# Mixers of a two-block transformer kernel on one core: the first dilated pair ahead of the last two delta heads

## The chip, the cores and the metric

One Trainium2 chip, one of its cores. The metric is the device time of one execution in microseconds (us). The kernel is built once and runs as one program.

## What is computed

The reference runs two blocks on a sequence of 1024 tokens of width 1024. The first has two hybrid layers (retention, neighbourhood attention, short convolution). The second, which the change touches, mixes tokens in two ways at once, and a projection, a normalisation and a feed-forward follow.

```python
h = rmsnorm(x, g_mix_pre)
proj = h @ w_in
qa, ka, va, gate_a, beta_a, alpha_a, qb, kb, vb = split(proj)
out_a = gated_deltanet(qa, ka, va, gate_a, beta_a, alpha_a, ...)   # 4 heads of 128
out_b = dilated_attention(qb, kb, vb, rel_bias)                    # 8 heads of 64, in 4 pairs
mix = concatenate([out_a, out_b]) @ w_out
x = x + rmsnorm(mix, g_mix_post)
```

A delta head takes its q, k and v through a causal convolution over 4 tokens and silu, normalises q and k, solves a triangular system in each chunk (t_inv), then runs a recurrence over the chunks (v_new, o_i, state), and is multiplied by silu of its gate at the end. A dilated pair is two heads of softmax attention under a mask and a bias.

## The kernel before

All matrices are fp32. Each projection splits both operands into a rounded fp32r part and a remainder and adds three products (`xh,wh`, `xl,wh`, `xh,wl`). The names: `xh`/`xl` are the hidden state, `wh`/`wl` a weight.

A **projection block** is `fm_block`: one 128-wide column block of `w_in` against all tokens, two groups of 24 matmuls with 512 columns, so 48 matmuls of one length. The mixers make 24 of them, in the order of the string `ORDER`. An item `c0` is delta head 0: three blocks (k, v, q), each followed by the convolution of that block (`conv_gen`, tiles `c2x`, `c2y`, mostly VectorE), and then the head itself, `gdn_gen`. An item `d0` is dilated pair 0: a block for keys (`dK`), a block for queries (`dQ`), then eight units (`dil_unit`). An item `g0` is the gate of delta head 0: one block, multiplied onto the finished head (`g2o`).

`gdn_gen` of a head is called here in three parts: the *recursion* (31 pairs of a VectorE multiply into `Tt` and a VectorE reduction into `T`, each of which needs the one before), the *solve* (some 120 small fp32 matmuls and their evictions: `Y`, `Z`, `YT`, `gk`, `gv`, `kbe`), and the *scan* over 8 chunks (`vn`, `Sg`: TensorE and VectorE in turns). A `dil_unit` computes scores (TensorE), adds bias `dB` and takes the maximum while reading PSUM (VectorE, the tile `dsl`), exponentiates (ScalarE), scales (VectorE), transposes (TensorE), splits the transposed block (`pt`: ScalarE, then VectorE) and multiplies with the values `dv` (TensorE).

The engines run their rows strictly in the order in which they stand. That order is set when the kernel is built: `Mixer` holds a clock of its own, steps the waiting generators (heads, units, convolutions) between the matmuls of the projection blocks, and gives each row a rank. So `ORDER` decides in which projection blocks a head or a unit can be interleaved. `ROOM` and `need_room` wait for free tiles before a pair starts; `need2` makes the gate of a head wait for the head.

Weights are fetched two blocks ahead by SyncE's queue (`wr`), split by ScalarE (`wh`) and GpSimd (`wl`), in the same order as the blocks (`weights2` reads `ORDER` too). After the mixers `after_mix` multiplies with `w_out` (first rows: `wh,yhl`).

Of the kernel before, what the change touches and what calls it, by code (L numbers as in the profile page):

```python
# [1679 lines left out]
class Block2(Layers):  # L1680
# [18 lines left out]
    def weights2(self):  # L1699
        io = self.io  # L1700
        self.down_weights(io["w_vb2"], self.token_groups(0))
        w = io["w_in2"]
        for s in self.ORDER.split():
            i = int(s[1])
# [46 lines left out]
    def mixers(self, hT):  # L1751
# [23 lines left out]
        self.left = {}  # L1775
        order = self.ORDER.split()
        for n, s in enumerate(order):
# [23 lines left out]
                self.gate2_block(i, gx)  # L1801
        self.free(*hT.tiles())

    ORDER = "c0 c1 c2 c3 d0 g0 d1 g1 d2 d3 g2 g3"
    ROOM = 6
    CG = 4
    CA = 3
# [884 lines left out]
```

## Time and profile before

| | us |
|---|---|
| median of 3 runs | 2977.12 (2975.47 to 2979.05) |
| the profiled execution | 2977.17 |
| its span, first to last instruction | 2975.4 |
| TensorE busy in the span | 2724.7 (92%) |
| VectorE busy in the span | 1999.8 (67%) |
| the mixers' stretch of the span | 1552 to 2174 |

The span is what the trace shows; 1.8 us lie around it. The granted TensorE clock is given as a share of full speed; a stretch at 0.5 ran at 1.2 GHz, one at 1.0 at 2.4 GHz, and values between are means over both. Busy TensorE at half clock does half the work.

### The profile page before, as it was taken

Reading aid. Unit: us, or ns where it says so; the run is one execution under the profiler, and the core shown is the slowest. Engines: PE = TensorE matmul, PEld = TensorE weight load, DVE = VectorE, ACT = ScalarE, POOL = GpSimd, SP = SyncE. Lnnn points to the kernel's source line nnn. Section 1 sums busy time; section 2 is a strip of 40 time slices with the busy share of each in tenths; the row PEclk is TensorE's granted clock in tenths of the full one; section 3 lists DMA queues with packets and bytes.
Section 4 is the critical chain, followed back from the end, with each engine's and each line's share of the span. In section 5 each row is a group of like instructions: output and inputs, shape, how many; then the busy total and the mean of one; then the engine's idle time right before and its main releaser. Section 6 shows DMA issues by size and latency. Waiting matters only on the chain. (4 is left out here: it accounts for less than half of the span.)

```text
span 2975.4 us, 41142 instructions
## 1 busy us (share of the span) xinstructions
PE 2724.7 (92%) x14508; PEld 2340.2 (79%) x14508; DVE 1999.8 (67%) x3985; ACT 1200.1 (40%) x2745; POOL 975.0 (33%) x830
## 2 busy tenths in 40 slices
PE   6989999999879989999889968798998799999997
PEld 6978888888779878888787757687776688887885
DVE  7866776684642557665554887777744877876786
ACT  5222254553442225554444323455544333333443
POOL 4343512213443441222563321110135644443001
PEclk9989999999989999999999979998998899999998
DMA  7534202225333221224543433221353122223874
GB/s 268 178 101 120 91 24 89 78 76 198 114 99 102 64 68 36 95 81 142 171 131 117 162 130 116 86 86 53 107 170 137 69 106 107 107 106 143 299 234 156
DMA packets 170480, 358.44 MB, mean 120 GB/s; under 512 B 29761, under 2 KB 57697, under 8 KB 170273
## 3 DMA queue, kind: packets, MB, share of 16 engines
q1 hardware_dynamic: 157472, 333.63, 33.2%
q10 hardware_dynamic: 10016, 13.12, 1.8%
q0 software_dynamic: 2784, 9.05, 1.0%
q8 instruction: 115, 1.88, 0.3%
q14 instruction: 93, 0.75, 0.1%
HBM read 274.11 MB, written 75.32 MB: 117 GB/s over the span
## 5 line engine op out<-in xcount | busy, mean ns | idle before, releaser
L251 POOL TENSOR_TENSOR wl<-wr,wh 128x512 fp32r<-128x512 f32 (+2 forms) x344 | 459.3, 1339 | 1177.9 <-ACT wh L251 1086.3
L344 PE MATMUL pb<-xl,wh 128*128 128x512 f32 x1456 | 579.7, 398 | 0.0
L344 PE MATMUL pb<-xh,wl 128*128 128x512 f32 x1456 | 579.1, 398 | 0.0
L344 PE MATMUL pb<-xh,wh 128*128 128x512 f32 x1456 | 578.9, 398 | 0.0
L251 ACT ACTIVATE wh<-wr 128x512 fp32r<-128x512 f32 (+2 forms) x344 | 203.6, 594 | 419.1 <-PE pb L344 331.0
L344 PEld LDWEIGHTS pb<-xh,wl 128*128 128x128 f32 x1456 | 277.6, 191 | 56.0 <-issue 0.6
L344 PEld LDWEIGHTS pb<-xl,wh 128*128 128x128 f32 x1456 | 278.0, 191 | 54.7 <-issue 0.2
L344 PEld LDWEIGHTS pb<-xh,wh 128*128 128x128 f32 x1456 | 277.9, 191 | 53.3 <-issue 0.3
L344 PE MATMUL pb<-wh,yhl 128*128 128x512 f32 x832 | 267.9, 401 | 15.8 <-DVE lr L251 6.9
L344 PE MATMUL pb<-T,wh 128*128 128x512 f32 x640 | 198.0, 391 | 15.3 <-DVE T L251 15.3
L344 PEld LDWEIGHTS pb<-wh,yhl 128*128 128x128 f32 x832 | 160.6, 194 | 51.4 <-issue 8.0
L251 POOL TENSOR_TENSOR wl<-ws,wh 128x512 fp32r<-128x512 f32 x100 | 137.1, 1371 | 137.7 <-ACT wh L251 133.8
L344 PE MATMUL pb<-wl,yhl 128*128 128x512 f32 x416 | 166.4, 400 | 6.3 <-POOL wl L251 6.3
L344 PE MATMUL pb<-whi,yhl 128*128 128x512 f32 x528 | 163.8, 391 | 4.5 <-DVE yhl L251 4.5
L251 ACT ACTIVATE pt<-pb 128x512 fp32r<-128x512 f32 (+3 forms) x230 | 114.9, 528 | 123.8 <-PE pb L349 121.7
L251 DVE TENSOR_TENSOR pt<-pb,pt 128x512 fp32r<-128x512 f32 (+3 forms) x230 | 129.4, 595 | 51.2 <-ACT pt L251 50.5
L344 PEld LDWEIGHTS pb<-T,wh 128*128 128x128 f32 x640 | 120.5, 189 | 40.8 <-DVE T L251 15.7
L251 DVE TENSOR_TENSOR yhl<-yr,yhl 128x512 fp32r<-128x512 f32 (+2 forms) x133 | 99.1, 771 | 60.0 <-ACT yhl L251 59.6
L344 PE MATMUL pb<-wl,xh 128*128 128x384 f32 (+1 forms) x384 | 126.3, 329 | 6.5 <-POOL wl L251 6.5
L251 ACT ACTIVATE wh<-ws 128x512 fp32r<-128x512 f32 x100 | 63.2, 632 | 168.4 <-PE pb L344 167.6
L344 PE MATMUL pb<-wh,xl 128*128 128x384 f32 (+1 forms) x384 | 125.4, 327 | 3.3 <-ACT wh L251 1.4
L344 PE MATMUL pb<-T,wl 128*128 128x512 f32 x320 | 125.0, 390 | 0.0
(432 smaller groups left out, 6020.8 us busy)
## 6 DMA issues: line engine op xcount, KB each, us to landing
wr<-in_w_in_dram SPq DMA_DIRECT2D x152, 256.0 KB, 2.7
ws<-in_w_down_dram SPq DMA_DIRECT2D x110, 256.0 KB, 5.0
wr<-in_w_out_dram SPq DMA_DIRECT2D x96, 256.0 KB, 2.9
yr<-ffn SPq DMA_DIRECT2D x33, 512.0 KB, 5.9
wm<-in_w_modT_dram SPq DMA_DIRECT2D x32, 512.0 KB, 4.3
wr<-in_w_v_dram SPq DMA_DIRECT2D x64, 192.0 KB, 2.4
ws<-in_w_gate_dram SPq DMA_DIRECT2D x22, 512.0 KB, 5.2
ws<-in_w_up_dram SPq DMA_DIRECT2D x22, 512.0 KB, 5.6
```

Source lines behind the costliest of these rows:

```text
L251: return fn(*a, **kw)
L344: self.mix.product(c / 2.4, out, (lhsT, rhs), lambda: self.nc.tensor.matmul(out, lhsT, rhs, start=start, stop=stop))
```

## The change

The order of the items changes, and nothing else: pair 0 comes after two delta heads instead of after four. `weights2` reads the same string, so that the weights come in the new order too.

```diff
-    ORDER = "c0 c1 c2 c3 d0 g0 d1 g1 d2 d3 g2 g3"
+    ORDER = "c0 c1 d0 c2 c3 g0 d1 g1 d2 d3 g2 g3"
```

Each engine keeps the same matmuls and evictions; 11891 printed rows stand on TensorE in both programs. The first six blocks (c0, c1) are where they were. Three places show what moved.

**VectorE, at the start of head 0's recursion** (`T`, `Tt`; `c2y` is a convolution, `dK` the keys of pair 0, `rr` a norm of head 1). Before:

```order
L251 TENSOR_SCALAR rr_3315_16212<-pb_16203 128x8
L251 TENSOR_TENSOR rr_3315_16212<-rr_3315_16212,egc 128x8
L251 SCALAR_TENSOR_TENSOR c2y_16093<-c2x_16092,conv_13771,c2y_16093 128x1023
L251 COPY T_16303<-tini 128x256
L251 SCALAR_TENSOR_TENSOR c2y_16093<-c2x_16092,conv_13771,c2y_16093 128x1022
L251 TENSOR_TENSOR Tt_16305<-T_16303,nd_16164 128x8x2
L251 SCALAR_TENSOR_TENSOR c2y_16093<-c2x_16092,conv_13771,c2y_16093 128x1021
L251 TENSOR_REDUCE T_16303<-Tt_16305 128x8
```

And in the changed kernel:

```order
L251 TENSOR_SCALAR rr_3315_16211<-pb_16202 128x8
L251 TENSOR_TENSOR rr_3315_16211<-rr_3315_16211,egc 128x8
L251 TENSOR_TENSOR dK_3297_16092<-pb_16106,dK_3297_16092 64x512
L251 TENSOR_TENSOR dK_3298_16093<-pb_16106,dK_3298_16093 64x512
L251 TENSOR_TENSOR dK_3297_16092<-pb_16187,dK_3297_16092 64x512
L251 TENSOR_TENSOR dK_3298_16093<-pb_16187,dK_3298_16093 64x512
L251 COPY T_16309<-tini 128x256
L251 TENSOR_TENSOR Tt_16311<-T_16309,nd_16164 128x8x2
L251 TENSOR_REDUCE T_16309<-Tt_16311 128x8
```

The convolutions of heads 2 and 3 left this place and pair 0's keys came to it. From the copy into `T` to the first score of pair 0 there are now 60 of the recursion's 62 rows, 1 row of a convolution, 4 of `dQ`, 4 of `dv`, 5 of the heads and 1 of `dB`.

**TensorE, after head 1's first products** (`gq`, `gk`). Before, projections of head 2 follow:

```order
L344 MATMUL pb_16438<-gq_16273,gk_16271 128x128 x4
L344 MATMUL pb_16453<-gk_16271 128x128 x4
L344 MATMUL pb_16454<-gq_16273,gk_16271 128x128 x4
L344 MATMUL pb_16405<-xl_14687,wh_16338 128x512
L344 MATMUL pb_16405<-xh_14683,wh_16338 128x512
L344 MATMUL pb_16405<-xh_14683,wl_16339 128x512
```

In the changed kernel the scores of pair 0 follow, 16 rows of them, and then its transpositions:

```order
L344 MATMUL pb_16386<-gq_16277,gk_16275 128x128 x4
L344 MATMUL pb_16405<-gk_16275 128x128 x4
L344 MATMUL pb_16406<-gq_16277,gk_16275 128x128 x4
L344 MATMUL pb_16429<-dK_3297_16092,dQ_3316_16229 128x512
L344 MATMUL pb_16429<-dK_3297_16092,dQ_3318_16231 128x512
L344 MATMUL pb_16438<-dK_3297_16092,dQ_3316_16229 128x512
L344 MATMUL pb_16438<-dK_3297_16092,dQ_3318_16231 128x512
```

No projection stands between the heads' products and the scores, and the next projections (head 2's) come behind the first values of the pair.

**TensorE, at the mixers' end** (`wh,yhl` is the output projection's first matmul, `pb_21036` in the rows of before the last gate's projection). Before:

```order
L344 MATMUL pb_21036<-xl_14688,wh_20836 128x512
L344 MATMUL pb_21036<-xh_14684,wh_20836 128x512
L344 MATMUL pb_21036<-xh_14684,wl_20837 128x512
L344 MATMUL pb_21073<-pt_21053,dv_20428 128x256 x2
L344 MATMUL pb_21073<-pt_21053,dv_20428 128x128 x2
L344 MATMUL pb_21086<-wh_20842,yhl_21095 128x512
```

In the changed kernel:

```order
L344 MATMUL pb_21053<-pt_21010,dv_20428 128x256 x2
L344 MATMUL pb_21053<-pt_21010,dv_20428 128x128 x2
L349 MATMUL pb_21066<-ident,dsl_21028 128x128 x3
L344 MATMUL pb_21073<-pt_21070,dv_20428 128x256 x2
L344 MATMUL pb_21073<-pt_21070,dv_20428 128x128 x2
L344 MATMUL pb_21086<-wh_20624,yhl_21095 128x512
```

The last projection moved ahead: 88 rows of the last pair's units (36 transpositions, 44 products with values, 8 scores) now stand behind it, where before 4 did.

What stands on TensorE beside the projections, block by block, in rows of the printed order (the block counted is the one that ends there):

| blocks | before, other rows | changed, other rows |
|---|---|---|
| 1 to 8 | 56 | 56 |
| 9 | 25 | 176 |
| 10 and 11 | 9 | 257 |
| 12 to 18 | 738 | 101 |
| 19 | 176 | 381 |
| 20 to 24 and after | 404 | 437 |

## Rows read from the trace of the kernel before

**Rows 1.** The page's first section: busy time, share of the span, instructions.

```profile
PE 2724.7 (92%) x14508; PEld 2340.2 (79%) x14508; DVE 1999.8 (67%) x3985; ACT 1200.1 (40%) x2745; POOL 975.0 (33%) x830
```

**Rows 2.** Windows over the mixers: length, busy time by engine, granted clock, DMA.

```profile
1552.00:1658.00 106.00, 96.44 (x444) 80.50 (x443) 56.97 (x83) 41.15 (x77) 34.28 (x22) 0.92 0.40 133
1658.00:1690.00 32.00, 31.93 (x166) 26.78 (x165) 28.65 (x58) 10.46 (x18) 9.93 (x8) 1.00 0.48 163
1690.00:1808.00 118.00, 83.41 (x428) 72.12 (x426) 104.31 (x206) 32.19 (x68) 32.30 (x28) 0.79 0.43 146
1808.00:1892.00 84.00, 76.35 (x546) 66.17 (x544) 65.09 (x157) 34.92 (x94) 15.97 (x16) 0.97 0.30 99
1892.00:1949.00 57.00, 45.43 (x338) 40.49 (x339) 41.15 (x130) 29.66 (x79) 7.58 (x9) 0.88 0.16 52
1949.00:1988.00 39.00, 38.21 (x206) 31.68 (x205) 20.43 (x38) 19.95 (x52) 7.59 (x6) 1.00 0.34 115
1988.00:2051.00 63.00, 55.00 (x314) 47.09 (x312) 46.90 (x138) 36.50 (x81) 9.92 (x8) 0.97 0.22 72
2051.00:2117.00 66.00, 61.54 (x328) 53.61 (x329) 47.88 (x141) 39.14 (x83) 7.07 (x6) 0.90 0.20 64
2117.00:2174.00 57.00, 45.84 (x265) 38.94 (x264) 45.95 (x136) 32.52 (x72) 5.24 (x4) 0.94 0.34 111
1552.00:2174.00 622.00, 534.16 (x3025) 457.38 (x3023) 457.32 (x1080) 276.50 (x623) 129.87 (x105) 0.91 0.33 108
```

**Rows 3.** The same view, 20 us inside the third stretch.

```profile
1740.00:1760.00 20.00, 11.51 (x68) 10.55 (x69) 15.98 (x31) 3.60 (x10) 3.58 (x2) 0.57 0.39 138
```

**Rows 4.** TensorE's timeline from 1640 to 1684: start, length, operation, count.

```profile
1645.11 0.48 PE L344 MATMUL pb<-xh,wh 128*128 128x512 f32 x1
...
1652.70 0.39 PE L344 MATMUL pb<-xh,wh 128*128 128x512 f32 x1
1652.93 1.84 PE L344 MATMUL pb<-ones,c2x 128*128 128x1 f32 x16
...
1678.43 1.05 PE L344 MATMUL pb<-gk 128*128 128x128 f32 x8
...
1681.32 1.06 PE L344 MATMUL pb<-gq,gk 128*128 128x128 f32 x8
```

**Rows 5.** The tile T: its first copy on VectorE.

```profile
L251 DVE COPY T<-tini x4: 273/276/327, 1659.4 to 1841.4; 128x256 f32<-128x256 f32 x4
```

**Rows 6.** VectorE's groups from 1552 to 2174: count, busy us, mean ns, idle before.

```profile
L251 DVE TENSOR_TENSOR Tt<-T,nd 128x216 f32<-128x216 f32 (+30 forms) x124 | 61.9, 503 | 4.7 <-POOL nd L251 2.2
L251 DVE CUSTOM_DVE_ANT_0 dsl<-pb,dB 128x512 f32<-128x512 f32 (+2 forms) x96 | 51.0, 548 | 3.1 <-PE pb L344 2.8
L251 DVE SCALAR_TENSOR_TENSOR c2y<-c2x,conv,c2y 128x1023 f32<-128x1023 f32 (+2 forms) x36 | 49.5, 1376 | 10.4 <-ACT c2y L251 10.1
L251 DVE TENSOR_TENSOR pt<-pb,pt 128x512 fp32r<-128x512 f32 (+1 forms) x80 | 47.8, 630 | 16.0 <-ACT pt L251 15.6
L251 DVE TENSOR_REDUCE T<-Tt 128x8 f32<-128x216 f32 (+30 forms) x124 | 35.9, 293 | 2.7
L251 DVE TENSOR_SCALAR dsl<-dsl,rsm 128x896 f32<-128x896 f32 (+3 forms) x64 | 33.3, 562 | 0.6
...
L251 DVE TENSOR_TENSOR dQ<-pb,dQ 64x512 fp32r<-64x512 f32 x16 | 11.0, 688 | 7.2 <-ACT dQ L251 6.9
L251 DVE TENSOR_TENSOR dv<-dvr,dv 128x256 fp32r<-128x256 f32 x16 | 10.8, 732 | 4.2 <-ACT dv L251 4.1
L251 DVE SCALAR_TENSOR_TENSOR dB<-dB,dilm 128x1024 f32<-128x1024 f32 x8 | 9.7, 1224 | 2.9 <-DMA dB<-in_rel_dram 2.9
...
L251 DVE TENSOR_TENSOR vn<-gv,pb 128x128 f32<-128x128 f32 x28 | 7.9, 282 | 11.2 <-PE pb L344 11.2
...
L251 DVE TENSOR_TENSOR YT<-YT,pb 128x512 f32<-128x512 f32 x8 | 5.5, 688 | 2.7 <-PE pb L344 2.5
...
L251 DVE TENSOR_SCALAR nmx<-nmx 128x1 f32<-128x1 f32 x32 | 4.6, 146 | 0.1
```

## The prediction

> **What bounds the kernel now.** I read the page first: TensorE is busy for 92% of the span, VectorE for 67%, the others far less [rows 1]. So the question is what TensorE loses, and where. The change stays inside the mixers, from 1552 to 2174 us, so I cut these 622 us into stretches and looked at each in the view of windows [rows 2]. For each I work out TensorE's **loss**: length less busy time times granted clock, which takes idle time and time at half clock together. The nine stretches lose 17.3, 0.1, 52.1, 9.9, 17.0, 0.8, 9.7, 10.6 and 13.9, together 131.4 us (the first: 106 - 96.44 x 0.92). What is left, 622 - 131.4 = 490.6, is TensorE's work at full clock. The change adds and removes no matmul, so this work stays, and the whole prediction is about the 131.4.
>
> The reader should see two kinds of stretch. From 1949 to 1988 projections stand between the steps of a scan, and TensorE loses 0.8 of 39 us while VectorE is busy for half. From 1690 to 1808 VectorE is busy 104.31 of 118 us and TensorE loses 52.1: two delta heads and the convolutions of two more are on VectorE, and TensorE has few projections left to put between. There VectorE sets the pace; nearly everywhere else TensorE does.
>
> **The change part by part.** Projections run 34 in 7.82 us, 0.23 each [rows 4]; 24 blocks of 48 are 265 us. The remaining 226 us are 1408 other rows, 0.16 us each on average. With that and the table by blocks I price TensorE's work in each new stage; VectorE's comes from its groups [rows 6].
>
> *A, up to the end of head 1's convolutions.* The order is the same: loss 17.3 as before.
>
> *B, the wait for pair 0's first score.* TensorE stands at 1645.1 after head 0's products [rows 4]. Then come 89 projections (20.5 us), 8 sums (1.84), head 1's products (1678.43 to 1682.4, so 4.0) and a transposition (0.3): done at 1671.7. VectorE starts the recursion at 1659.4 [rows 5] and must finish, before it reads the first score, 60 of a head's 62 recursion rows ((61.9 + 35.9)/4 = 24.5 us a head, so 23.4 without the longest two), one convolution row 1.4, four `dQ` 2.8, four `dv` 2.9, one copy and four evictions 3.0, one `dB` 1.2: 34.7 us [rows 6], so 1694.1. TensorE idles 22.4 us, less some 2.6 for the 16 score rows that fit into PSUM ahead: loss 20. Before, this time was covered by head 2's projections: 31.93 of 32 us busy, clock 1.00 [rows 2]. This is the surest term. At 0.884 busy, as in the third stretch, VectorE is 4.6 us later and the loss 24; if half the evictions slip behind the first score it is 15.
>
> *C, half of pair 0 with the rest of both recursions*, until head 2's first block is through. TensorE: 48 projections and 176 other rows, 11 + 28 = 39 us. VectorE: 12 scores 6.6, 16 small rows of 0.146 2.3, 59 recursion rows 23.3, 8 scalings 4.5, 10 `pt` 6.3, three `tmpo` and a `dB` 2.4, 14 rows of the heads at 0.5 (between 0.28 of `vn` and 0.69 of `YT`) 7.0: 52.4 us [rows 6]. As dense as in the third stretch (104.31/118 = 0.884 [rows 2]) this is 59 us. VectorE bounds it: loss 59 - 39 = 20. Without any gap it would be 13.
>
> *D, the scans of heads 0 and 1 between head 2's blocks.* TensorE 96 projections and 257 others, 63 us; VectorE some 63 (14 convolution rows 19, 12 scores and what follows 24, 50 small rows of the heads 20). Both near the bound: 63/0.884 = 71, loss 8. If it packs as from 1949 to 1988, loss 1; nearest to a scan under projections, but with more on VectorE, so I keep 8.
>
> *E, seven almost pure blocks, 12 to 18.* 336 projections and 101 others: 93 us of TensorE with VectorE half idle. The loss lies between 2% (1949 to 1988) and 16% (the first stretch, also projections with convolutions behind them): 2 to 15, I take 8.
>
> *F, block 19: pair 1, the solve and scan of head 2, the recursion and solve of head 3.* TensorE 48 projections and 381 others, 72 us. VectorE: 24 scores 13.2, 32 small rows 4.7, 62 recursion rows 24.5, 16 scalings 9.0, 20 `pt` 12.6, 8 `tmpo` 3.4, gate and keys 5.5, 51 rows of the heads at 0.4 20.4: 93.3 us. At the third stretch's density 105.5 us, loss 33; at that of 1892 to 1949, which is the same mixture (a pair and a head's scan, VectorE busy 41.15 of 57 [rows 2]), 129 us, loss 57; without a gap 21. I take 38, nearer to the density that carried more VectorE work. Before, this lump held 313 other rows in block 16 and had 2.7 blocks of projections around it.
>
> *G, the scan of head 3 under projections:* 2, as from 1949 to 1988.
>
> *H, pairs 2 and 3 with the last gates.* Three pairs lost 9.7 + 10.6 + 13.9 = 34.2 before [rows 2]; two lose 22.8. But at the end 43 projections (9.9 us) that filled the waits of the last units now stand ahead of them, and 88 rows come behind the last projection with nothing to fill. Of the 9.9 I take 7 as new loss: 30 (bounds 23 and 33).
>
> The sum: 17.3 + 20 + 20 + 8 + 8 + 38 + 2 + 30 = 143.3, against 131.4. That is 11.9 us more on the profiled execution's 2977.17 (span 2975.4 and 1.8 around it; the median is 2977.12, the same within 0.1): 2989.1. A change of 0.2%, 6 us, is about what can be told from none here.
>
> **A rule on the clock.** From 1740 to 1760 TensorE was busy 11.51 of 20 us, after gaps, at a granted clock of 0.57, mostly 1.2 GHz [rows 3]; over the third stretch it did 65.9 us of work in 118, 0.56 a microsecond. C needs 39 in 59, 0.66. At 0.56 C takes 70 us instead of 59, 11 more.
> The Trainium skill's page "TensorE: Matmul & The Clock Gate", Part 1, says that the half clock is what an idle array has, and that activity lifts it; the rows agree. By that rule at its worst, all of C at half clock, C's 39 us would take 78, 19 more than in the sum.
>
> **The rivals.** *Faster: the freed projections pay.* The third stretch lost 52.1 because the projections of heads 2 and 3 had been used up when the scans of heads 0 and 1 needed filling. Now nine blocks stand among and behind them. If D and E lose 3 and 2, C and F run without gaps on VectorE (14 and 21) and H loses 25, the losses are 17.3 + 20 + 14 + 3 + 2 + 21 + 2 + 25 = 104.3, 27.1 less than before: 2950. It decides at F: under some 95 us for block 19 the kernel is faster. For it: VectorE is busy for only 457.32 of 622 us, so there is room. Against it: the units and the heads wait on each other row by row, and 15.6 us before `pt` were spent waiting for ScalarE [rows 6]. Half of this gain gives 2964.
>
> *No change: the losses only move.* F at 33, E at 5, H at 23, D at 5 give 125 to 129, so 2971 to 2975; with one more term as forecast it is within 6 us of before. For it: total work of every engine is unchanged.
>
> *Slower by more: TensorE falls to half clock in both VectorE-bound stages.* At 0.56 of work a microsecond C takes 70 and F 129 us: losses 31 and 57, 30 more than forecast, 3019. It needs TensorE to be starved for as long as in the third stretch, twice.
>
> That the change does nothing is excluded: from block 9 on the orders differ.
>
> **How the numbers follow.** Slower by the sum, 0.40, and by the clock in addition, 0.12: 0.52. Within 6 us: 0.24. Faster: 0.24, half of it down to 2964. The time is that of the sum, 2989. For the range I leave out the outer half of the faster case and the far end of the clock case: 2964 to 3010. The forecast case alone spans 2983 to 3001.
>
> **What the changed profile would show.** B right: TensorE idle for some 20 us about 1672 to 1694, its clock near half there. C and F right: two stretches where VectorE is above 0.85 busy and TensorE's work is under 0.7 of the time, of some 59 and 110 us. E right: some 90 to 100 us of projections at full clock. H right: TensorE with gaps between the last projection and the output projection. The mixers should end about 2186 instead of 2174, and what follows should take the same. Wrong would be: scans so well filled that block 19 is through in under 95 us; or a weight that arrives late because its fetch stands behind the pair's stores on SyncE.

## The result and the profile after

The changed kernel takes 2999.55 us (median of 5 runs, 2991.60 to 3001.38), the kernel before 2979.05 beside it (5 runs, 2975.47 to 2981.66). The ratio is 1.0068, with a 95% interval of 1.0055 to 1.0081: some 20 us slower, where 11.9 were forecast. The profiled execution has a span of 2997.7 us, 22.3 more than before.

The page's first section, which answers to [rows 1]: TensorE is as busy as before, to within 8 us.

```profile
PE 2732.4 (91%) x14508; PEld 2348.6 (78%) x14508; DVE 1992.0 (66%) x3985; ACT 1201.1 (40%) x2745; POOL 975.4 (33%) x830
```

The windows over the mixers, cut at the ends of the prediction's stages A, B, C, D, E (two rows), F, G and H (two rows); columns as in [rows 2].

```profile
1552.00:1669.00 117.00, 107.95 (x494) 89.85 (x492) 66.39 (x106) 43.93 (x85) 39.71 (x27) 0.93 0.39 131
1669.00:1695.00 26.00, 9.56 (x48) 8.78 (x48) 24.58 (x54) 6.13 (x13) 3.67 (x2) 0.67 0.53 183
1695.00:1746.00 51.00, 36.91 (x233) 32.83 (x234) 44.59 (x137) 18.70 (x41) 4.79 (x7) 0.80 0.22 67
1746.00:1824.00 78.00, 71.61 (x474) 62.44 (x472) 54.02 (x126) 40.59 (x104) 14.60 (x14) 0.93 0.25 81
1824.00:1916.00 92.00, 84.92 (x413) 71.80 (x414) 58.75 (x90) 33.34 (x68) 36.13 (x23) 0.94 0.43 144
1916.00:1948.00 32.00, 22.95 (x97) 18.88 (x96) 29.30 (x72) 10.86 (x21) 4.39 (x7) 0.84 0.47 161
1948.00:2052.00 104.00, 83.39 (x572) 74.50 (x571) 73.48 (x206) 41.25 (x103) 12.37 (x12) 0.87 0.18 56
2052.00:2069.00 17.00, 16.08 (x85) 12.73 (x85) 6.93 (x17) 9.09 (x27) 2.57 (x2) 1.00 0.40 140
2069.00:2177.00 108.00, 95.80 (x536) 82.53 (x535) 80.58 (x237) 60.59 (x135) 15.12 (x12) 0.94 0.27 90
2177.00:2197.00 20.00, 12.43 (x89) 10.40 (x88) 16.38 (x46) 13.39 (x34) 1.61 (x1) 0.98 0.28 82
```

The losses (length less busy time times granted clock) are 16.6, 19.6, 21.5, 11.4, 12.2 and 12.7, 31.5, 0.9, 17.9 and 7.8: 152.1 us, against 131.4 before. The work is 645 - 152.1 = 492.9. The mixers end at 2197 instead of 2174, and what follows takes as long as before.

A sum of losses does not say where the two kernels part, since the same work stands in another order. For that I add up TensorE's work and ask when each kernel has done the same amount: after's from the rows above, before's from [rows 2], in proportion inside a row.

| work done, us | changed, at | before, at | changed is |
|---|---|---|---|
| 106.8 (end of B) | 1695 | 1676 | 19 behind |
| 136.3 (end of C) | 1746 | 1718 | 28 behind |
| 202.9 (end of D) | 1824 | 1827 | 3 ahead |
| 282.7 (in E) | 1916 | 1924 | 8 ahead |
| 302.0 (end of E) | 1948 | 1950 | 2 ahead |
| 374.5 (end of F) | 2052 | 2030 | 22 behind |
| 390.6 (end of G) | 2069 | 2049 | 20 behind |
| 480.7 (in H) | 2177 | 2161 | 16 behind |
| the end | 2197 | 2174 | 23 behind |

Such a count has an error. The matmuls of all the orders in this document are the same, and yet their work, added up in windows of 10 us, comes to anything from 493 to 504 us. So I read a row of the table as good to some 5 us; that is an estimate from these sums.

The wait for pair 0 costs what was forecast, and all of it is paid back by 1824: in the kernel before the third stretch of [rows 2] loses 52.1 us at the same point of the work. **The change is lost in F, from 1948 to 2052**, where heads 2 and 3 meet pair 1. Behind F, by this count, 6 us come back, and the last 20 us, without projections, cost 7.

From 1948 to 2014 no projection stands on TensorE. The same view of that stretch:

```profile
1948.00:2014.00 66.00, 49.46 (x345) 45.02 (x344) 57.99 (x181) 29.51 (x74) 6.14 (x7) 0.85 0.17 50
```

Before, the stretch in which a pair runs without projections lies at 1887 to 1948, with pair 0:

```profile
1887.00:1948.00 61.00, 48.08 (x360) 42.76 (x359) 45.18 (x133) 30.40 (x80) 8.87 (x10) 0.89 0.18 56
```

It held the last 4 reductions of head 3's recursion. In the changed kernel all 31 of head 3 stand in it. The rows that read the tile `Tt` (and write `T`) from 1948 to 2014 in the changed kernel (count, shortest, median and longest ns, first and last start):

```profile
L251 DVE TENSOR_REDUCE T<-Tt x31: 158/297/417, 1948.3 to 2005.9; 128x8 f32<-128x16 f32 x1, 128x8 f32<-128x24 f32 x1, 128x8 f32<-128x32 f32 x1, 128x8 f32<-128x40 f32 x1
```

VectorE is 88% busy there instead of 74%, and TensorE loses 24.0 us instead of 18.2. Ahead of it, from 1824 to 1916, VectorE was idle for 33 of 92 us.

### The profile page after: what moved, and what is told of

The parts are those of the page before. It is cut to its first block, busy times and chain, and to the rows that moved or that the text cites. A ratio compares the mean times of both kernels' runs of the same rounds, so it can differ in the third digit from the quotient of the medians.

```text
span 2997.7 us, 41145 instructions
## 1 busy us (share of the span) xinstructions
PE 2732.4 (91%) x14508; PEld 2348.6 (78%) x14508; DVE 1992.0 (66%) x3985; ACT 1201.1 (40%) x2745; POOL 975.4 (33%) x830
## 5 line engine op out<-in xcount | busy, mean ns | idle before, releaser
L344 PEld LDWEIGHTS pb<-T,wh 128*128 128x128 f32 x640 | 120.5, 189 | 41.6 <-DVE T L251 16.6
L344 PE MATMUL pb<-wh,xh 128*128 128x384 f32 (+1 forms) x384 | 125.0, 326 | 0.0
```

What stands on the lines that cost most here:

```text
L344: self.mix.product(c / 2.4, out, (lhsT, rhs), lambda: self.nc.tensor.matmul(out, lhsT, rhs, start=start, stop=stop))
```

## The experiments

All times are set against the kernel before on the same chip; 0.1% is 3 us. The intervals reach some 0.1 to 0.2% to each side, so two of the ratios must differ by about 0.2% (5 us) to be told apart. Five theories came up in turn: the recursion on VectorE ahead of a pair's scores (1, later B), the end that lacks projections (2, later Q), the loads of q and k (3), the stage with heads 2, 3 and pair 1 (E, R), and the break in the run of heads (P).

**One head ahead of pair 0 instead of two.**

```diff
-    ORDER = "c0 c1 d0 c2 c3 g0 d1 g1 d2 d3 g2 g3"
+    ORDER = "c0 c1 c2 d0 c3 g0 d1 g1 d2 d3 g2 g3"
```

> The dilated pair 0 is moved ahead of one delta head instead of two (c0 c1 c2 d0 c3 ...). Theory 1 (a pair is dear where its first scores stand on VectorE behind a whole triangular recursion): in this order both recursions of heads 0 and 1 are done before pair 0's first scores, and head 2's starts after them, so the wait at the start of the pair should be gone and the time should be 2970 to 2983 us, at most 4 us from the kernel before. Theory 2 (a pair that is taken from the end costs, wherever it goes, because the end has fewer projections and TensorE is granted less clock): about half of the change's +20 us, 2985 to 2992 us.

Measured: 3009.01 us, ratio 1.0107 (1.0089 to 1.0125), slower than the change itself. Both theories missed. TensorE's timeline has two waits of 17.7 us, the first of them here (idle time ahead and its cause in brackets):

```profile
1743.11 3.78 PE L344 MATMUL pb<-Y,nbr 128*128 128x128 f32 x16 [17.69 <-ACT Y L251]
```

The solves of heads 0 and 1 stand there with few projections between. From 1715 to 1820 TensorE does this much:

```profile
1715.00:1820.00 105.00, 61.65 (x404) 54.31 (x404) 76.29 (x172) 24.80 (x62) 14.23 (x16) 0.76 0.32 107
```

That is a loss of 58.1 in 105 us. The kernel before loses nearly as much in the same stretch:

```profile
1715.00:1820.00 105.00, 73.86 (x452) 65.21 (x451) 86.69 (x180) 26.99 (x62) 23.52 (x21) 0.79 0.40 136
```

That is 46.7, with waits of 11.1 and 9.6 us. So these two waits explain little of this order's price. Counted by equal work, in windows of 10 us, it is 3 us ahead of the kernel before at 1922, 2 behind at 1950 and 23 behind at 2015. It falls behind where the changed kernel does, while head 3's recursion (1943 to 2029) and pair 1 stand on VectorE. A wait at the pair's start is not needed for the order to be dear.

**Shorter recursions**, in both orders, for all heads and for heads 2 and 3 alone. The ranks are those of the full size; the rows for heads 2 and 3 use `k = i + 1 if h < 2 else 2`.

```diff
-            self.tt(tmp[:, :, 0:i + 1], T[:, :, 0:i + 1], ndT[:, i:i + 1, 0:i + 1]..., ALU.mult)
-            v.tensor_reduce(T[:, :, i], tmp[:, :, 0:i + 1], ...)
+            v.eng.tensor_tensor(tmp[:, :, 0:2], T[:, :, 0:2], ndT[:, i:i + 1, 0:2]..., op=ALU.mult)
+            v.eng.tensor_reduce(T[:, :, i], tmp[:, :, 0:2], ...)
```

> The kernel before, with the recursion's rows cut to two columns each (31 multiplies and 31 sums per head stay, with 128x8x2 elements), which leaves out most of the triangular solve. Order of instructions as before. VectorE loses about 10 to 15 us of work per head. Theory 1 (VectorE's order sets the stalls): the kernel before loses little in its recursions, since projections cover them: 2955 to 2972 us. Theory 2 (VectorE's total is what counts): nearer to all of the removed work, 2930 to 2950 us. It is the partner of the next run, and their difference is what counts.

> The changed kernel with the same cut (two columns per row of the recursion, most of the solve left out), instructions in the changed kernel's order. Theory 1 (the changed kernel loses where a pair's scores stand behind a recursion, around 1669 to 1746 us and again around 1916 to 1960 us): it gains more from the cut than the kernel before does, so the difference to the run before shrinks from 20 us to under 10 us. Theory 2 (the loss is the last stretch without projections, or the granted clock, or the loads of q and k that TensorE waits for): the difference stays at 15 to 25 us.

> The changed kernel with the recursion cut to two columns per row for heads 2 and 3 alone (most of their triangular solve is left out; heads 0 and 1 are solved in full), in the changed kernel's order. The cut on all four heads was worth about 25 us. Theory E (the change loses where heads 2 and 3 meet pair 1, about 1860 to 2050 us, and the wait at pair 0's start only takes the place of waits that the kernel before has at 1715 to 1820 us): this half of the cut gives 15 us or more, 2976 to 2982 us. Theory B (the loss is the stretch 1669 to 1746 us, where pair 0 waits behind head 0's recursion): it gives 10 us or less, 2987 to 2994 us.

> The kernel before with the recursion cut to two columns per row for heads 2 and 3 alone (most of their triangular solve is left out), the partner of the run that did the same to the changed kernel and gained about 16 us there; all four heads' cut gained about 27 us in the kernel before and 25 us in the changed one. Theory E (the kernel before pays for VectorE in heads 0 and 1, at 1715 to 1820 us, and the changed kernel in heads 2 and 3, where pair 1 lies beside them): the cut on heads 2 and 3 gives 10 us or less here, 2968 to 2976 us against 2978. Rival (a recursion costs the same 6 to 7 us in both orders, and the change's price lies in something else): 12 us or more, 2960 to 2966 us.

| cut | kernel before | changed kernel | difference |
|---|---|---|---|
| none | 1 | 1.0068 (1.0055 to 1.0081) | 0.0068 |
| heads 2 and 3 | 0.9964 (0.9950 to 0.9978) | 1.0012 (1.0003 to 1.0020) | 0.0048 |
| all heads | 0.9910 (0.9895 to 0.9925) | 0.9985 (0.9973 to 0.9998) | 0.0075 |

The medians with the cut are 2968.47 and 2982.35 us for heads 2 and 3, 2951.57 and 2970.34 for all; 2951.57 lies between the two forecasts of its run. With all recursions cut the difference stays as it was (18.8 us by the medians), as theory 2 expected, so theory 1 falls: the length of the recursion ahead of pair 0 is not the price. Of the waits at pair 0's start the first stays and the second is halved (12.39 and 11.73 without the cut); TensorE's timeline of the changed kernel with the cut:

```profile
1670.86 2.05 PE L344 MATMUL pb<-gk 128*128 128x128 f32 x8 [4.03 <-DMA gk<-pscr]
1685.35 2.04 PE L344 MATMUL pb<-gq,gk 128*128 128x128 f32 x8 [12.44 <-DMA gq<-pscr]
1700.46 0.47 PE L349 MATMUL pb<-ident,dsl 128*128 128x128 f32 x1 [6.29 <-DVE dsl L251]
```

The recursions of heads 2 and 3 are worth 0.56% (17 us) in the changed kernel and 0.36% (11 us) in the kernel before; what is left for heads 0 and 1 is 0.27% in the changed kernel and 0.54% before. That is theory E's pattern, but 0.20% is no more than the intervals allow, and its bound of 10 us for the kernel before was met by the medians (9.5 us) and just missed by the ratio (10.7): an indication.

**The loads of q and k.** The last multiply of heads 1's and 3's query convolution goes to GpSimd; its rank stays.

```diff
-            self.tt(y, y, x, ALU.mult)
+            if b in (1, 3):
+                nc.gpsimd.eng.tensor_tensor(y, y, x, op=ALU.mult)
+            else:
+                self.tt(y, y, x, ALU.mult)
```

> The changed kernel, where the last multiply of heads 1's and 3's query convolution runs on GpSimd instead of VectorE, where it stood behind 33 rows of a recursion; all other orders stay but for a few rows that shift by one or two places. It lets the query reach memory, and be loaded by TensorE's next product, earlier. Theory 3 (the new loss is TensorE's wait for these loads, 12.4 us at 1686 and 4.9 us at 1923): 8 to 15 us less than the changed kernel, 2984 to 2992 us. Theory 1 (behind that wait stands the next one, pair 0's first scores, which VectorE reaches only after its recursion): TensorE only waits at the next instruction instead, and the time is 2996 to 3001 us, within 4 us of the changed kernel.

Measured: 2996.61 us, ratio 1.0064 (1.0049 to 1.0078), the same as the change. TensorE at the pair's start, first in the changed kernel:

```profile
1686.06 2.05 PE L344 MATMUL pb<-gq,gk 128*128 128x128 f32 x8 [12.39 <-DMA gq<-pscr]
...
1706.22 0.48 PE L349 MATMUL pb<-ident,dsl 128*128 128x128 f32 x1 [11.73 <-DVE dsl L251]
```

and with the multiply on GpSimd:

```profile
1679.59 2.05 PE L344 MATMUL pb<-gq,gk 128*128 128x128 f32 x8 [10.61 <-DMA gq<-pscr]
...
1685.34 2.23 PE L344 MATMUL pb<-dK,dQ 128*128 128x512 f32 x10 [1.24 <-ACT dQ L251]
1688.80 1.70 PE L344 MATMUL pb<-dK,dQ 128*128 128x512 f32 x6 [1.23 <-DVE gcr L251]
1702.93 0.47 PE L349 MATMUL pb<-ident,dsl 128*128 128x128 f32 x1 [12.43 <-DVE dsl L251]
```

From head 1's first products (1672.5 and 1667.9) to these transpositions it is 33.7 us without and 35.1 with the move: the first wait gives 1.8 us, the second takes 0.7 of them, and two waits of 1.2 us stand between that were not there. At the second place, where the changed kernel waits 4.9 us for `gq` at 1923, the load's wait is gone and a wait of 4.9 us for `dQ` (ScalarE) stands in its stead. So theory 1's forecast for this run came true and theory 3's 8 to 15 us did not, though at the first place the move took away only 1.8 of the 12.4 us that it was meant to test. The Trainium skill's page "GPSIMD Engine Reference", §3.1, has GpSimd about twice as slow as VectorE on work with two inputs; the rows agree (2.49 us against 1.22 for 128x1024), and the time does not show it.

**TensorE's idle time and its clock.** 24 products more after pair 0's first scores, into a bank that is overwritten.

```diff
             ps = self.bank()
+            if m == 3 and h == 0 and gi == 0 and self.left[0] == 8:
+                for j in range(24):
+                    self.nc.tensor.matmul(ps, Kt[:, 0:128], Q[:, 0:512], start=(j == 0), stop=(j == 23))
```

> The changed kernel with 24 more products of 128x512 on TensorE after pair 0's first scores (their result is overwritten), where it waits 11.9 us for VectorE; all other rows of TensorE keep their order. They take 5 us at full clock and 10 us at half. If TensorE only waits there: within 2 us of the changed kernel, 2995 to 3000 us. If the low granted clock behind the wait (0.79 to 0.80 up to 1746 us) is part of the price and work in the wait keeps it up: 2 to 6 us less, 2991 to 2995 us. If TensorE is what bounds that stretch: 5 to 10 us more.

Measured: 2999.61 us, ratio 1.0066 (1.0053 to 1.0079): no difference from the change that can be told. The added rows in TensorE's timeline, and stage C in the windows:

```profile
1703.72 8.03 PE L2029 MATMUL pb<-dQ,dK 128*128 128x512 f32 x24 [5.34 <-DVE dmx L251]
```

```profile
1695.00:1746.00 51.00, 42.60 (x258) 36.52 (x257) 44.27 (x139) 17.50 (x39) 2.89 (x6) 0.87 0.24 68
```

TensorE takes 8.03 us more and is granted 0.87 instead of 0.80, and the stage ends no earlier for it: the projections behind the transpositions start at 1718.7 instead of 1715.7, 3.0 us later, and head 1's products ahead of them stood 4.0 us later already. VectorE, 44.27 of 51, sets it. That activity lifts the clock is what the Trainium skill's page "TensorE: Matmul & The Clock Gate", Part 1, says, and the rows agree. But the lower clock was no part of the price that these runs can tell.

**Where the gates stand beside pair 1.** Two orders against the changed one:

```diff
-    ORDER = "c0 c1 d0 c2 c3 g0 d1 g1 d2 d3 g2 g3"
+    ORDER = "c0 c1 d0 c2 c3 d1 g0 g1 d2 d3 g2 g3"
```

```diff
-    ORDER = "c0 c1 d0 c2 c3 g0 d1 g1 d2 d3 g2 g3"
+    ORDER = "c0 c1 d0 c2 c3 g0 g1 d1 d2 d3 g2 g3"
```

> Order c0 c1 d0 c2 c3 d1 g0 g1 d2 d3 g2 g3: against the changed kernel pair 1's two blocks trade places with gate 0's, so one more block of projections is left to lie beside pair 1 and the end of heads 2 and 3, and pair 1 can start while VectorE is half idle. Theory E (the stretch 1860 to 2050 us lacks projections for TensorE and gathers VectorE's work): 4 to 12 us less than the changed kernel, 2985 to 2993 us. Rival (pairs that come earlier cost, whatever lies beside them): 2997 to 3005 us.

> Order c0 c1 d0 c2 c3 g0 g1 d1 d2 d3 g2 g3: against the changed kernel gate 1 goes ahead of pair 1, so pair 1 starts later, behind more of the recursions of heads 2 and 3, and one block of projections fewer lies beside pair 1. Theory E, if the lack of projections is what costs: 3 to 10 us more than the changed kernel, 3000 to 3007 us. If the meeting of pair 1 with the recursions is what costs: 4 to 12 us less, 2985 to 2993 us.

Measured: 3001.09 us, 1.0074 (1.0059 to 1.0088), and 2997.93 us, 1.0062 (1.0050 to 1.0074). Neither differs from the change. One projection block more or less beside pair 1 makes no difference, which theory E in its first form had claimed. The second run's other forecast, that less meeting of pair 1 with the recursions gives 4 to 12 us back, missed as well.

The trace of the first of them speaks against that meeting as the cause. There head 3's recursion runs from 1941.6 to 1969.8, and pair 1's scores are read up to 1938.6 and then from 1993.4 on. So hardly anything of the pair lies beside the recursion, and yet TensorE stands still: it needs `Z`, a row of another head's solve (head 3's own comes after its `T`), and that row stands in VectorE's order behind all but the last row of this recursion. A window of 10 us, and the matmul that ends the wait:

```profile
1952.00:1962.00 10.00, 0.00 (x0) 0.00 (x0) 9.14 (x26) 0.00 (x0) 0.00 (x0) 0.50 0.00 1
```

```profile
1969.30 1.11 PE L344 MATMUL pb<-Z,YT 64*64 64x64 f32 x8 [20.69 <-DVE Z L251]
```

By equal work this order is 4 us ahead of the kernel before at 1944 and 21 behind at 1982. As much is lost at the same place without the pair's scores.

**Pairs at other places.** These three tell the last theories apart:

```diff
-    ORDER = "c0 c1 d0 c2 c3 g0 d1 g1 d2 d3 g2 g3"
+    ORDER = "d0 c0 c1 c2 c3 g0 d1 g1 d2 d3 g2 g3"
```

```diff
-    ORDER = "c0 c1 d0 c2 c3 g0 d1 g1 d2 d3 g2 g3"
+    ORDER = "c0 c1 d0 c2 d1 c3 g0 g1 d2 d3 g2 g3"
```

```diff
-    ORDER = "c0 c1 c2 c3 d0 g0 d1 g1 d2 d3 g2 g3"
+    ORDER = "c0 c1 c2 c3 d0 d1 g0 g1 d2 d3 g2 g3"
```

> Order d0 c0 c1 c2 c3 g0 d1 g1 d2 d3 g2 g3: pair 0 goes ahead of all delta heads, which follow one another without a break as in the kernel before. Theory P (the change breaks the run of four delta heads in two: the four heads' preparation, recursion, solve and scan are started and drained twice, and each start and drain leaves TensorE without products): no break, so 2970 to 2986 us, at most 8 us from the kernel before. Rival Q (a pair taken from the end costs wherever it goes, since fewer projections are left for later): 2993 to 3005 us, as in the changed kernel.

> Order c0 c1 d0 c2 d1 c3 g0 g1 d2 d3 g2 g3: pair 1 goes between heads 2 and 3, a second break in the run of heads. Theory P: two breaks cost more than one, 3008 to 3030 us. Rival R (the changed kernel's price is that pair 1 lies beside the solves and scans of both heads 2 and 3 while VectorE stood half idle before): pair 1 comes earlier and meets less of them, 2985 to 2997 us.

> Order c0 c1 c2 c3 d0 d1 g0 g1 d2 d3 g2 g3: against the kernel before, pair 1 trades places with gate 0, and the run of heads stays whole. Theory P: 2970 to 2984 us. Rival Q (pairs that come earlier cost): 2984 to 2995 us. Should it be under 2970 us, it beats both kernels.

Measured: 2971.71 us, 0.9976 (0.9966 to 0.9985); 2986.49 us, 1.0028 (1.0018 to 1.0039); 2973.57 us, 0.9984 (0.9972 to 0.9996).

The first and the last beat both kernels, as theory P forecast for them, and theory Q falls: a pair may come earlier, even before all heads, and pay. The two breaks cost 0.28%, less than the one break's 0.68%, so P does not hold as a price per break; pair 1 between heads 2 and 3 gives 0.40% (12 us) back, as R expected. But a weaker P stands: every order here that keeps the run of heads whole takes 0.9976 to 1 of the time before, and every one that breaks it 1.0028 to 1.0107.

In the order with two breaks pair 1's last score is read at 1938.6, and head 3's recursion starts at 2010.7. So pair 1 is kept away from head 3's recursion, and pair 2, whose scores start at 2024.7, stands beside it instead. The stretch without projections (2017 to 2083) is no better than the changed kernel's:

```profile
2017.00:2083.00 66.00, 42.55 (x251) 36.89 (x250) 56.95 (x179) 31.12 (x71) 4.78 (x7) 0.79 0.10 33
```

A loss of 32.4. What it gains seems to lie ahead of that, where pair 1 runs beside head 3's projections; from 1824 to 1916 and 1916 to 1948:

```profile
1824.00:1916.00 92.00, 81.15 (x440) 68.90 (x439) 64.22 (x170) 45.36 (x100) 21.52 (x17) 0.96 0.32 107
1916.00:1948.00 32.00, 30.13 (x165) 25.19 (x164) 31.25 (x67) 16.99 (x40) 5.85 (x5) 1.00 0.37 118
```

VectorE does 95.5 us there instead of 88.1, and TensorE loses 16.0 instead of 24.9, though this order's work comes to some 10 us more than the others', so its losses are the least certain. (The profiled repetition is the longest of this kernel's 12; its span is 6.4 us under the changed one's.)

With pair 0 ahead of all heads VectorE has more to do in the first stretch, where it is half idle otherwise, and TensorE loses 9.1 there instead of 16.6:

```profile
1552.00:1669.00 117.00, 111.19 (x589) 94.61 (x587) 84.02 (x203) 64.74 (x135) 32.95 (x22) 0.97 0.31 105
```

## Why the prediction was right in direction and short in size

The sum of losses was to rise from 131.4 to 143.3; it rose to 152.1. E's term alone was 16.9 us short. That the sum is off by only 8.8 is luck in part: F was put 6.5 and H 4.3 us too high. The other 2.3 us of the 23 by which the mixers end later are in the work (492.9 against 490.6).

- **A, B, C, G hold in size:** 17.3, 20, 20, 2 forecast; 16.6, 19.6, 21.5, 0.9 found. B came by another way. TensorE did not wait only behind the scores: before them it stood for 12.4 us at head 1's products, for `gq`, whose convolution's last multiply stands inside the recursion on VectorE, and behind them for 11.7 more. These two waits lie on either side of 1695, so only B and C together are a fair test: 41.1 for 40. VectorE reads the first score at 1698.90 instead of 1694.1, which is where the variant at 0.884 busy had put it:

```profile
1698.90 0.68 DVE L251 CUSTOM_DVE_ANT_0 dsl<-pb,dB 128x512 f32<-128x512 f32 x1
```

  C's loss is luck in part. TensorE's work in it was 29.5 us and not 39, VectorE's 44.6 and not 52.4, and the stage took 51 us and not 59; the errors cancel in the difference.
- **D** lost 11.4 for 8.
- **E is the step that failed:** "seven almost pure blocks, 12 to 18 ... with VectorE half idle", 8 us. It lost 24.9. Up to 1916 VectorE was indeed idle for a third of the time and more (busy 58.75 of 92), and TensorE lost 12.2, inside the range of 2 to 15 for the whole stage but already above the 8 taken for it. In the last 32 us, which lost the other 12.7, VectorE was busy for 29.30: head 2's recursion and head 3's convolution stand ahead of what head 3's products and pair 1's scores need, as in B. TensorE's longest waits from 1916 to 2052 (total, times, longest, us); those for `gq` and `dmx` lie in E, the other two in F:

```profile
PE pb L344 <- DVE vn L251: 7.6, 2, 4.7
PE pb L344 <- DMA gq<-pscr: 4.9, 1, 4.9
PE pb L349 <- DVE gv L251: 3.7, 1, 3.7
PE pb L344 <- DVE dmx L251: 3.2, 1, 3.2
```

  I had counted B's situation once; the order makes it twice, the second time smaller. The block count (101 other rows in seven blocks) hid it, because it counts TensorE's rows and the wait comes from VectorE's.
- **F** lost 31.5 for 38 in 104 us. The announced sign, VectorE above 0.85 busy throughout, is wrong: 0.88 up to 2014, and then, with projections again, it has little to do. In C it is right (44.59 of 51).
- **H** lost 25.7 for 30: fewer projections at the end cost less than forecast.

*Faster* was to be decided by block 19 in under 95 us; it took 104. *Slower by the clock* needed 70 and 129 us for C and F (51 and 104 found), and the added products show no gain from the clock in C. No weight came late: none of TensorE's waits in the mixers is for one.

Shown: by equal work the changed kernel falls behind in F and not, on balance, at pair 0's start. Filling TensorE's idle time in C, shortening all recursions and moving the gates leave the time or the difference as it is, and a pair that comes early does not cost by itself. That the loads are not the price is likely, but only a part of their wait was tested.

Open: what makes F dear. My theory was that head 3's recursion and pair 1 share VectorE in a stretch without projections, after VectorE stood half idle. For it speaks that pair 1 ahead of head 3 gave back 12 of 20 us, and that the cut of heads 2 and 3 gave six more here than before, which is within the intervals. Against it speaks the order with pair 1 ahead of the gates, in which TensorE stands idle for 20.7 us behind head 3's recursion without pair 1 beside it, and which takes as long as the changed kernel. Where pair 1 was kept away from head 3's recursion by the order, pair 2 took its place. A rival is that head 3's recursion comes when too few projections are left for TensorE. In the kernel before and in the order with pair 0 first, TensorE runs 71 and 73 projections during that recursion, and loses 8.1 us in 54 and 7.2 in 38; in the changed kernel it runs 3, and loses 18.0 in 58. But with one head ahead of pair 0 it runs 131 in 87 us and that order is the slowest, and with pairs 0 and 1 right behind the heads it runs 23 in 54 and that order is fast. So the rival is no full account either, and no run was made to test it.

## What to carry over

When only the order changes, compare the two traces at equal work done, not at equal time or by sums of losses, and find out from kernels of equal work how far such a count can be trusted: 24 us of new waits (12.4 and 11.7) can be free because old ones go, and the price can come 250 us later. Look for where the second engine is idle while the first is full, since that time may come back as a stretch where the second sets the pace; the order that uses it (a pair ahead of all heads) is 0.24% faster than the kernel before. And when a wait is priced for one place, look for every place in the order that has the same neighbours.

## What the hardware showed unexpectedly

A higher granted clock can be worth nothing: 24 products of 128x512 in 8.03 us raised it from 0.80 to 0.87 over 51 us, and the time did not change (ratios of 1.0066 and 1.0068 to the kernel before). A chain through DRAM takes long: from the store of a head's row norms (1662.3) over the broadcast, the multiply, the store and the load to the product that uses it (1686.06) passed 24 us. Not all of it is transfer: the broadcast row was loaded 4.1 us after its issue at 1665.7, and the multiply came at 1677.9, in its place in VectorE's order. From the store of the product (1679.1) to its use passed 7 us, 3.9 of them from the issue of the load of 512 KB to its landing.
